# One layer of a hybrid recurrent backbone: the order of HGRN's logarithms, and a power on GpSimd for two token norms

## The chip, the cores and the metric

The kernel runs on one core of one Trainium2 chip. The metric is the device time of one execution in microseconds (us). The engines are named as in the profile: PE is TensorE's matmuls, PEld its weight loads, DVE is VectorE, ACT is ScalarE, POOL is GpSimd, and SP (SyncE) issues most transfers. PE's clock has two levels, 1.2 and 2.4 GHz; the profile gives the granted clock of a stretch as a share of the higher one.

## The reference

One layer on 640 tokens (128 of context, 512 latent) with 1024 channels: a modulated RMS norm, one wide projection, three recurrent mixers (HGRN2, RWKV-7, mLSTM), a gated merge, an output projection, and a SwiGLU feed-forward block. The change concerns HGRN's forget gates, and the RMS norm of each token over the 128 channels of a head, which HGRN and mLSTM both have:

```python
def _rms(x, w, eps=RMS_EPS):
    x32 = x.astype(F32)
    y = x32 * lax.rsqrt(jnp.mean(x32 * x32, axis=-1, keepdims=True) + eps)
    return (y * w.astype(F32)).astype(x.dtype)
...
    for d, fpre in enumerate((hf_fwd, hf_bwd)):
        z = fpre.astype(F32)
        logf = jnp.logaddexp(log_lb, log_ub + jax.nn.log_sigmoid(z)).reshape(B, T, HA, DKA)
        k = ((1.0 - lb) * jax.nn.sigmoid(-z)).reshape(B, T, HA, DKA)
...
    o = _rms(outs[0] + outs[1], norm_w.reshape(HA, DVA)).reshape(B, T, WA)
    return o * jax.nn.silu(hg.astype(F32)), jnp.stack(finals, axis=1)
...
    h = _rms(hs[0] + hs[1], norm_w.reshape(HC, DHC)).reshape(B, T, WC)
    return h * jax.nn.sigmoid(mo.astype(F32)), (jnp.stack(Cs, axis=1), jnp.stack(ns, axis=1), jnp.stack(ms, axis=1))
```

Both mixers have four heads of 128 channels, each run in both directions of time (fwd and bwd).

## The kernel before, in words

Channels lie on the partitions and the 640 tokens along the free axis, in two halves of 320; where a step needs tokens on the partitions, PE transposes blocks of 128x128 (`htr`, `hotr`, `mhtr`, `btr`). A projection multiplies in split floats: ACT casts a piece of a weight to its high part (`whi`, L344), DVE makes the low part (`wlo`, L262), and PE runs three products for each block of 128 channels (`pj<-h_hi,whi`, `h_lo,whi`, `h_hi,wlo`, all in the helper `mm`, L277). Four pairs of `whi` and `wlo` exist at a time; their sources `raw` are loaded by SP (`wload`, L332).

The stages, by their place in the span: modulation and the first norm up to 40 us; RWKV to about 605; the gates of mLSTM; from about 620 to 1010 the four heads of HGRN and of mLSTM, side by side; the merge with `ya`, `yc` and `hl` to 1100; the output projection with its norm (`rstd_rows`, L1519) to about 1235; the feed-forward block; the last norm.

In the stage of the heads two generators, `mlstm()` and `hgrn()`, are woven, a step of one after some steps of the other, and `fill()` lays projections between them that nothing in the heads waits for: the gates (their evacuation is L572, a Tanh, from PSUM to `gs`; L573 writes `gs` to DRAM, one half at a time, and two `gs` exist) and a part of the modulation of the next block (`acc`, `col`). `FILL2` sets how much fill goes to each head. The program order that comes out of this is a priority only: a list scheduler places the instructions on each engine in a fixed order before the kernel runs, by when it reckons their inputs to be there, and on the chip each engine keeps that order, an instruction waiting in front of all behind it. `tc.issue_after(x)` adds one rule to the scheduler: on x's engine what stands in the block comes after x. A table load of ACT is put in where two neighbours in ACT's final order need different tables.

A head of HGRN (`hgrn_head`): projections, then for each direction the gate's logarithm through Abs, Exp and Ln (L1096 to L1100), k through an Exp (L1107), a scan (L1110), Exps for the chunk states (`kh` L1118, `hqe` L1121, `heb` a copy on POOL); the transposes `htr`, their copy `hkt` (L1138), the states `hpr`; seven levels of pairs of Exp (`T1`, `T2`, L1193 and L1194, whose inputs POOL and DVE subtract, L1189 on) with products `hg`; the output `hop`, its copy to `o` and the sums of squares by ACT (L1222, `hssq`, 128 tokens by 5 chunks), the root and the reciprocal (L1223, L1224), the scaling of the five chunks (L1226), the transposes `hotr` (L1236), and `ya`, its high part by ACT (L1052) and its low part by DVE.

A head of mLSTM (`mlstm_head`): projections, `mkt` (L558, the copy of k's transposes), products `ms`, an Exp (`mD`, L1367), numerators `np` and `nq`, their copy `nd` (L1394), the division, sums of squares (L1413, `ssq`), root and reciprocal (L1414, L1415), the scaling (L1417), the transposes `mhtr` and `yc`.

Of the kernel before, what the change touches and what calls it, by code (L numbers as in the profile page):

```python
# [8 lines left out]
F32 = mybir.dt.float32  # L9
# [3 lines left out]
AF = mybir.ActivationFunctionType  # L13
ALU = mybir.AluOpType
# [88 lines left out]
COL_EPS6, COL_EPS64, COL_9LN2, COL_SEL = 0, 1, 2, 3  # L103
# [152 lines left out]
def build(tc, **A):  # L256
    nc = tc.nc
    dve, act, pe, pool, sp = nc.vector, nc.scalar, nc.tensor, nc.gpsimd, nc.sync
# [8 lines left out]
    def stt(out, a, s, b, op0, op1):  # L267
        dve.scalar_tensor_tensor(out, a, s, b, op0, op1)

    def ts(out, a, s1, s2=None, op0=ALU.mult, op1=ALU.add):  # L270
        if s2 is None:
            dve.tensor_scalar(out, a, s1, None, op0)
        else:
            dve.tensor_scalar(out, a, s1, s2, op0, op1)  # L274
# [18 lines left out]
    with ExitStack() as top:  # L293
# [22 lines left out]
        def col(i):  # L316
            return cols[:, i:i + 1]

        def P(n, i=0, w=1):
            return pcol[:, PC[n] + i:PC[n] + i + w]  # L320
# [724 lines left out]
        with ExitStack() as ms, ExitStack() as mr:  # L1045
# [18 lines left out]
            hb = ms.enter_context(tc.tile_pool(name="hb", bufs=1, reuse_waits="tile"))  # L1064
# [8 lines left out]
            ts(lb[:, 1], lb[:, 1], -1.0, 1.0)  # L1073
            rub = hb.tile([128, 4], F32, name="rub")
            dve.reciprocal(rub, lb[:, 1])
            hhn = hb.tile([128, 4], F32, name="hhn")
            ts(hhn, P("hn", 0, 4), 0.5)

            def hgrn_head(hd):
# [8 lines left out]
                b, kd, qe, SSs, zs, ls, khs, ebs = [], [], [], [], [], [], [], []  # L1088
# [5 lines left out]
                for d in D2:  # L1094
                    l = ht.tile([128, T], F32, name="hT2")
                    act.activation(l, zs[d], AF.Abs)  # L1096
                    act.activation(l, l, AF.Exp, scale=-1.0)
                    ls.append(l)
                for l in ls:
                    act.activation(l, l, AF.Ln, scale=rub[:, hd:hd + 1], bias=rub[:, hd:hd + 1])  # L1100
                yield
                for d in D2:
                    kk_ = hb.tile([128, T], F32, name=f"hk{d}")
                    bb = hb.tile([128, T], F32, name=f"hb{d}")
                    l = ls[d]
                    stt(kk_, zs[d], 0.0, l, ALU.max, ALU.add)
                    act.activation(kk_, kk_, AF.Exp, scale=-1.0)  # L1107
                    stt(l, zs[d], 0.0, l, ALU.min, ALU.subtract)
                    st = 1 if d == 0 else -1
                    dve.tensor_tensor_scan(bb[:, ::st], r128, l[:, ::st], 0.0, ALU.mult, ALU.add)  # L1110
                    b.append(bb)
                    kd.append(kk_)
                    yield
# [95 lines left out]
                ssq = hb.tile([128, 5], F32, name="hssq")  # L1209
                sq = hb.tile([128, 128], F32, name="hsq")  # L1210
                for c0, n in CP:
# [8 lines left out]
                    act.copy(o[:, c0:c0 + n], op[:, :n])  # L1220
                    for i in range(n):
                        act.activation(sq, op[:, i], AF.Square, accum_out=ssq[:, c0 + i:c0 + i + 1])  # L1222
                act.activation(ssq, ssq, AF.Sqrt, scale=1.0 / 128, bias=col(COL_EPS6))  # L1223
                dve.reciprocal(ssq, ssq)  # L1224
                for c in range(5):
                    (pool if c in HSP else dve).tensor_scalar(o[:, c], o[:, c], ssq[:, c:c + 1], None, ALU.mult)  # L1226
                hgr = ht.tile([128, T], F32, name="hT2")
# [106 lines left out]
            def mlstm():  # L1334
                yield from mlstm_gates()
                mr.close()
                mt = ms.enter_context(tc.tile_pool(name="mt", bufs=2, reuse_waits="tile"))
                for hd in range(4):
                    at[0] = hd
                    yield from mlstm_head(hd, mt)  # L1340

            def mlstm_head(hd, mt):
# [65 lines left out]
                ssq = mt.tile([128, 5], F32, name="ssq")  # L1408
                sq = mt.tile([128, 128], F32, name="msq")
                for c in range(5):  # L1410
                    ts(hh[:, c], nds[0][:, c, 0:128], rds[0][:, c:c + 1])
                    stt(hh[:, c], nds[1][:, c, 0:128], rds[1][:, c:c + 1], hh[:, c], ALU.mult, ALU.add)
                    act.activation(sq, hh[:, c], AF.Square, accum_out=ssq[:, c:c + 1])  # L1413
                act.activation(ssq, ssq, AF.Sqrt, scale=1.0 / 128, bias=col(COL_EPS6))  # L1414
                dve.reciprocal(ssq, ssq)  # L1415
                for c in range(5):
                    ts(hh[:, c], hh[:, c], ssq[:, c:c + 1])  # L1417
                og = mt.tile([128, T], F32, name="og", bufs=1)
# [11 lines left out]
            def hgrn():  # L1430
                for hd in range(4):
                    yield from hgrn_head(hd)
# [399 lines left out]
```

## Time and profile before

| what | value |
| --- | --- |
| median of 3 runs | 1620.4 us (1620.4 to 1620.68) |
| the profiled execution, its time | 1623.08 us |
| its span, first to last instruction | 1621.3 us |
| mean granted clock | 0.976 |
| PE busy | 1540.6 us, 95% of the span |
| DVE, ACT, POOL busy | 1131.9, 782.8, 275.7 us |

The span leaves out 1.8 us around the first and the last instruction. "Busy" counts an instruction from start to end, overlaps once; "idle before" is how long its engine stood, and the name behind the arrow is the instruction that ended it. Matmuls overlap, so a start says more about PE's pace than a duration does: neighbouring `pj` matmuls start 0.147 us apart at the full clock.

### The profile page before, as it was taken

To read this page: it belongs to the slowest core of one execution; us is meant where nothing else is said; L and a number is where in the kernel's file an instruction comes from. 1 tells how busy PE (TensorE), PEld (TensorE's weight loads), DVE (VectorE), ACT (ScalarE), POOL (GpSimd) and SP (SyncE) were. 2 spreads that over 40 slices of the span, in tenths; PEclk is the share of its full clock that TensorE was granted. 3 is DMA by queue.
4 is the path that set the end of the run, shared out by engine and by line. 5 is a ranking of instruction groups with operands and counts; after the bars stand their busy time and mean duration, and the time that the engine had idled before them with its cause. 6 is when DMAs were issued, how large, how long until landed. Compare 5 with 4: busy or idle time off the path is not lost. (4 is left out here: it accounts for less than half of the span.)

```text
span 1621.3 us, 34724 instructions
## 1 busy us (share of the span) xinstructions
PE 1540.6 (95%) x14194; PEld 1418.1 (87%) x14194; DVE 1131.9 (70%) x2355; ACT 782.8 (48%) x1546; POOL 275.7 (17%) x347
## 2 busy tenths in 40 slices
PE   6999999999999988899999999999999999999996
PEld 2988888888877778889798988999999999999996
DVE  6788788687777644786758578772887386586576
ACT  5364455454454334666476666223553343243244
POOL 2110110110110100211303031000123241341211
PEclk9999999999999969999999999999989999999998
DMA  9222222212122313232332332643512222222322
GB/s 361 71 75 88 74 71 80 95 50 88 66 73 95 113 49 103 70 99 78 94 100 85 100 101 95 201 145 108 155 37 86 95 79 76 82 88 68 99 94 97
DMA packets 63791, 157.35 MB, mean 97 GB/s; under 512 B 7432, under 2 KB 27912, under 8 KB 63504
## 3 DMA queue, kind: packets, MB, share of 16 engines
q1 hardware_dynamic: 63488, 155.13, 29.5%
q8 instruction: 111, 1.82, 0.5%
q14 instruction: 48, 0.39, 0.1%
q10 hardware_dynamic: 144, 0.00, 0.0%
HBM read 136.73 MB, written 18.37 MB: 96 GB/s over the span
## 5 line engine op out<-in xcount | busy, mean ns | idle before, releaser
L277 PE MATMUL pj<-h_hi,whi 128*128 128x320 f32 x1560 | 495.0, 320 | 5.4 <-ACT t L396 2.7
L277 PE MATMUL pj<-h_lo,whi 128*128 128x320 f32 x1560 | 494.4, 317 | 0.0
L277 PE MATMUL pj<-h_hi,wlo 128*128 128x320 f32 x1560 | 493.2, 317 | 0.0
L262 DVE TENSOR_TENSOR wlo<-raw,whi 128x512 fp32r<-128x512 f32 (+1 forms) x318 | 228.5, 726 | 130.7 <-ACT whi L344 106.2
L277 PEld LDWEIGHTS pj<-h_hi,whi 128*128 128x128 f32 x1560 | 296.3, 191 | 12.0 <-ACT t L396 3.7
L277 PEld LDWEIGHTS pj<-h_lo,whi 128*128 128x128 f32 x1560 | 296.7, 190 | 3.2
L277 PEld LDWEIGHTS pj<-h_hi,wlo 128*128 128x128 f32 x1560 | 296.9, 190 | 2.8
L344 ACT CAST whi<-raw 128x512 fp32r<-128x512 f32 (+1 forms) x264 | 156.8, 599 | 219.6 <-PE pj L277 209.4
L277 PE MATMUL pj<-a,whi 128*128 128x320 f32 x704 | 155.3, 309 | 0.0
L277 PEld LDWEIGHTS pj<-a,whi 128*128 128x128 f32 x704 | 117.7, 188 | 0.2
L277 PE MATMUL pj<-a,wlo 128*128 128x320 f32 x352 | 108.8, 309 | 0.0
L277 PE MATMUL pj<-t_hi,whi 128*128 128x320 f32 x288 | 89.1, 309 | 1.1 <-DVE u L262 1.1
L277 PE MATMUL pj<-t_hi,wlo 128*128 128x320 f32 x288 | 89.1, 309 | 0.1
L277 PE MATMUL pj<-t_lo,whi 128*128 128x320 f32 x288 | 89.0, 309 | 0.0
L262 DVE TENSOR_TENSOR wlo<-sm,whi 128x512 fp32r<-128x512 f32 x72 | 68.1, 946 | 11.4 <-ACT whi L1684 8.5
L1684 ACT CAST whi<-sm 128x512 fp32r<-128x512 f32 x72 | 44.4, 621 | 64.4 <-PE pj L277 50.2
L1678 POOL TENSOR_TENSOR sm<-raw 128x512 f32<-128x512 f32 x36 | 49.0, 1360 | 110.3 <-DMA raw<-wff 72.5
L277 PEld LDWEIGHTS pj<-a,wlo 128*128 128x128 f32 x352 | 66.1, 188 | 0.0
L277 PE MATMUL pj<-hl,whi 128*128 128x320 f32 x256 | 56.5, 310 | 0.6 <-ACT hl L1462 0.6
L1684 ACT CAST whi<-raw 128x512 fp32r<-128x512 f32 x54 | 33.5, 620 | 45.6 <-PE pj L277 37.7
L277 PEld LDWEIGHTS pj<-t_hi,whi 128*128 128x128 f32 x288 | 54.1, 188 | 1.3 <-DVE u L262 1.3
L277 PE MATMUL acc<-raw,sc 128*32 128x256 f32 (+1 forms) x320 | 40.7, 437 | 14.8 <-DMA raw<-wada 14.8
(659 smaller groups left out, 2988.0 us busy)
## 6 DMA issues: line engine op xcount, KB each, us to landing
raw<-wmix SPq DMA_DIRECT2D x76, 512.0 KB, 3.5
raw<-wada SPq DMA_DIRECT2D x48, 512.0 KB, 5.6
raw<-wff SPq DMA_DIRECT2D x44, 512.0 KB, 3.7
gates<-gs SPq DMA_DIRECT2D x64, 160.0 KB, 1.8
raw<-wff SPq DMA_DIRECT2D x24, 384.0 KB, 3.2
gs<-gates SPq DMA_DIRECT2D x24, 320.0 KB, 3.1
raw<-wbr SPq DMA_DIRECT2D x12, 512.0 KB, 4.3
raw<-wout SPq DMA_DIRECT2D x8, 512.0 KB, 5.0
```

What stands on the lines that cost most here:

```text
L262: dve.tensor_tensor(out, a, b, op)
L277: newest[0] = pe.matmul(out, lhsT=lhsT, rhs=rhs, start=start, stop=stop, skip_group_check=more).ins
L344: act.copy(hi[:, :w], raw[:, o:o + w])
L1678: pool.tensor_tensor(o, x, y, op)
L1684: act.copy(hi, x)
```

## The change

The first part is in HGRN's gate. Before, the two Ln are placed by the scheduler as their inputs come, each direction for itself, with other Exps between. Now both Ln may only follow the second direction's Exp (L1099 in the new numbering), and each Exp of hk (now L1112) only the second Ln. The second part is in both norms: `ssq` becomes `ssq`/128 + 1e-6 by a tensor_scalar on DVE, and POOL raises it to the power of a tile `mhalf` that holds -0.5, a tensor_tensor with the operation pow over 128x5. ACT's Sqrt (128x5) and DVE's reciprocal (128x5) go. `mhalf` is filled once by POOL.

```diff
             rub = hb.tile([128, 4], F32, name="rub")
             dve.reciprocal(rub, lb[:, 1])
+            mhalf = hb.tile([128, 5], F32, name="mhalf")
+            pool.memset(mhalf, -0.5)
...
                     act.activation(l, zs[d], AF.Abs)
-                    act.activation(l, l, AF.Exp, scale=-1.0)
+                    last = act.activation(l, l, AF.Exp, scale=-1.0).ins
                     ls.append(l)
-                for l in ls:
-                    act.activation(l, l, AF.Ln, scale=rub[:, hd:hd + 1], bias=rub[:, hd:hd + 1])
+
+                with tc.issue_after(last):
+                    for l in ls:
+                        last = act.activation(l, l, AF.Ln, scale=rub[:, hd:hd + 1], bias=rub[:, hd:hd + 1]).ins
                 yield
...
-                    act.activation(kk_, kk_, AF.Exp, scale=-1.0)
+                    with tc.issue_after(last):
+                        act.activation(kk_, kk_, AF.Exp, scale=-1.0)
...
-                act.activation(ssq, ssq, AF.Sqrt, scale=1.0 / 128, bias=col(COL_EPS6))
-                dve.reciprocal(ssq, ssq)
+                ts(ssq, ssq, 1.0 / 128, 1e-6)
+                pool.tensor_tensor(ssq, ssq, mhalf, ALU.pow)
                 for c in range(5):
                     (pool if c in HSP else dve).tensor_scalar(o[:, c], o[:, c], ssq[:, c:c + 1], None, ALU.mult)
...
-                act.activation(ssq, ssq, AF.Sqrt, scale=1.0 / 128, bias=col(COL_EPS6))
-                dve.reciprocal(ssq, ssq)
+                ts(ssq, ssq, 1.0 / 128, 1e-6)
+                pool.tensor_tensor(ssq, ssq, mhalf, ALU.pow)
                 for c in range(5):
                     ts(hh[:, c], hh[:, c], ssq[:, c:c + 1])
```

The lines of the new program are 2 to 5 higher than those of the old one for the same step. The scheduler places much of the stage of the heads anew. Three places:

ACT in head 0, from the second direction's `hqe` (the Exp of `hb`) to the copy `hkt`: L1118 and L1123 are the Exp of `kh`, L1193/L1194 and L1198/L1199 the Exps of T1 and T2. Before:

```order
L1121 ACTIVATE hqe_9011<-hb_8931 128x640
L396 ACTIVATE mq<-pj 128x320
L344 CAST whi<-raw 128x512
L1118 ACTIVATE hT_9007<-hT_9007 128x640
L1193 ACTIVATE hT_9124<-hT_9124 128x640
L1194 ACTIVATE hT_9125<-hT_9125 128x640
L396 ACTIVATE mk<-pj 128x320
L344 CAST whi<-raw 128x512
L1194 ACTIVATE hT_9199<-hT_9199 128x640
L1194 ACTIVATE hT_9235<-hT_9235 128x640
L396 ACTIVATE mk<-pj 128x320
L1138 COPY hkt<-htr 128x512
```

and now:

```order
L1126 ACTIVATE hqe_9013<-hb_8933 128x640
L396 ACTIVATE mk<-pj 128x320
L1198 ACTIVATE hT_9126<-hT_9126 128x640
L1123 ACTIVATE hT_9009<-hT_9009 128x640
L344 CAST whi<-raw 128x512 x2
L396 ACTIVATE mk<-pj 128x320
L1143 COPY hkt<-htr 128x512
L1198 ACTIVATE hT_9200<-hT_9200 128x640
L1199 ACTIVATE hT_9127<-hT_9127 128x640
L1199 ACTIVATE hT_9201<-hT_9201 128x640
```

Three Exps of T2 stood ahead of the copy; now they stand behind it.

PE at the end of head 0, where the five transposes `hotr` of HGRN's output stand among the fill (`pj`). Before, 21 fill matmuls come between the last `nq` of mLSTM and the first `hotr`; these are the last of them and what follows:

```order
L277 MATMUL pj<-h_lo,whi 128x320
L277 MATMUL pj<-h_hi,wlo 128x320
L277 MATMUL pj<-h_hi,whi 128x320
L277 MATMUL pj<-h_lo,whi 128x320
L1236 MATMUL hotr<-cst,hT_9477 128x128 x2
L277 MATMUL pj<-h_hi,wlo 128x320
L1236 MATMUL hotr<-cst,hT_9477 128x128 x2
L277 MATMUL pj<-h_hi,whi 128x320
L1236 MATMUL hotr<-cst,hT_9477 128x128
```

and now the whole way from that `nq` on:

```order
L277 MATMUL nq<-Cs,mq 128x129
L277 MATMUL pj<-h_hi,wlo 128x320
L277 MATMUL pj<-h_hi,whi 128x320
L277 MATMUL pj<-h_lo,whi 128x320
L277 MATMUL pj<-h_hi,wlo 128x320
L277 MATMUL pj<-h_hi,whi 128x320
L277 MATMUL pj<-h_lo,whi 128x320
L277 MATMUL pj<-h_hi,wlo 128x320
L277 MATMUL pj<-h_hi,whi 128x320
L1241 MATMUL hotr<-cst,hT_9479 128x128
```

Eight fill matmuls stand there instead of 21.

SP's queue in head 1, at the two gate transfers (`gates<-gs`) ahead of the state that HGRN writes out (`ohg`). Before:

```order
L332 DMA raw<-wmix 128x1024 x6
L573 DMA gates<-gs 128x320
L332 DMA raw<-wmix 128x1024
L573 DMA gates<-gs 128x320
L1147 DMA ohg<-hfs 128x128
```

and now:

```order
L332 DMA raw<-wmix 128x1024 x4
L573 DMA gates<-gs 128x320
L332 DMA raw<-wmix 128x1024
L573 DMA gates<-gs 128x320
L332 DMA raw<-wmix 128x1024
L1152 DMA ohg<-hfs 128x128
```

Each of the two gate transfers has passed one weight load, which now follows it.

## Rows read from the trace of the kernel before

**Rows 1.** The page's head, and busy time, share of the span and instructions of PE, PEld, DVE, ACT and POOL.

```profile
span 1621.3 us, 34724 instructions
PE 1540.6 (95%) x14194; PEld 1418.1 (87%) x14194; DVE 1131.9 (70%) x2355; ACT 782.8 (48%) x1546; POOL 275.7 (17%) x347
```

**Rows 2.** Busy time by stretches of 20 us through the stage of the heads: length; PE, PEld, DVE, ACT and POOL busy with their instructions; granted clock, DMA share, GB/s. The last row is the sum of all twenty from 620 to 1020.

```profile
640.00:660.00 20.00, 20.00 (x140) 19.99 (x139) 10.19 (x12) 14.60 (x24) 1.67 (x2) 1.00 0.25 79
...
720.00:740.00 20.00, 19.94 (x140) 19.50 (x139) 11.12 (x32) 13.77 (x30) 0.00 (x0) 1.00 0.33 108
...
sum 400.00, PE 380.29 PEld 358.69 DVE 282.36 ACT 246.81 POOL 71.95; mean PE 19.01 PEld 17.93 DVE 14.12 ACT 12.34 POOL 3.60
```

**Rows 3.** PE's waits from 620 to 1030: what waited, for whom; us in total, times, the longest.

```profile
PE nq L277 <- ACT nd L1394: 5.8, 6, 1.5
PE hpr L277 <- ACT hkt L1138: 5.4, 3, 5.0
PE ms L277 <- ACT mkt L558: 3.5, 3, 1.5
PE pj L277 <- DVE mod L262: 0.7, 1, 0.7
```

**Rows 4.** Groups of ACT's instructions by line and operation: busy time, mean ns of one, idle before.

```profile
L1100 ACT ACT_TABLE_LOAD x8 | 10.3, 1283 | 0.1
L1107 ACT ACT_TABLE_LOAD x8 | 10.3, 1283 | 0.1
...
L1223 ACT ACT_TABLE_LOAD x4 | 5.1, 1283 | 0.1
L1414 ACT ACT_TABLE_LOAD x4 | 5.1, 1283 | 0.1
L572 ACT ACT_TABLE_LOAD x4 | 5.1, 1283 | 0.4 <-DMA gates<-gs 0.4
```

**Rows 5.** ACT's timeline in head 0: start, duration, what, and the idle time before it with what ended it.

```profile
649.18 1.28 ACT L1100 ACT_TABLE_LOAD   x1
650.48 0.92 ACT L1100 ACTIVATE hT<-hT,rub 128x640 f32<-128x640 f32 x1
...
668.94 0.74 ACT L1194 ACTIVATE hT<-hT 128x640 f32<-128x640 f32 x1 [1.63 <-DVE hT L262]
...
672.33 1.54 ACT L1194 ACTIVATE hT<-hT 128x640 f32<-128x640 f32 x2 [1.82 <-DVE hT L262]
...
674.09 0.58 ACT L1138 COPY hkt<-htr 128x512 f32<-128x512 f32 x1
```

**Rows 6.** PE's longest wait in head 0, from its timeline, and two stretches of 2 us around it (columns as in Rows 2).

```profile
674.73 0.58 PE L277 MATMUL hpr<-hv,hkt 128*128 128x128 f32 x1 [4.96 <-ACT hkt L1138]
...
672.00:674.00 2.00, 0.00 (x0) 0.00 (x0) 2.00 (x5) 1.60 (x3) 0.00 (x0) 0.55 0.00 0
...
676.00:678.00 2.00, 2.00 (x10) 2.00 (x10) 1.16 (x4) 0.00 (x0) 0.00 (x0) 0.50 0.45 84
```

**Rows 7.** Timelines around `mkt`: SP's queue and ACT in head 1, then PE's first `ms` in heads 1, 2 and 3. For SP the duration is how long the transfer's issue stood in the queue.

```profile
765.23 7.30 SPq L332 DMA_DIRECT2D raw<-wmix  x2
772.62 0.38 SPq L573 DMA_DIRECT2D gates<-gs  x1
...
776.58 0.44 ACT L572 ACTIVATE gs<-pj 128x320 f32<-128x320 f32 x1 [2.61 <-DMA gates<-gs]
...
777.44 0.38 PE L277 MATMUL ms<-mq,mk 128*128 128x128 f32 x1 [1.47 <-ACT mkt L558]
869.64 0.38 PE L277 MATMUL ms<-mq,mk 128*128 128x128 f32 x1 [0.53 <-ACT mkt L558]
962.23 0.38 PE L277 MATMUL ms<-mq,mk 128*128 128x128 f32 x1 [1.52 <-ACT mkt L558]
```

**Rows 8.** Timelines at the end of head 0: the last read of a sum of squares and the table load on ACT; HGRN's scaling and mLSTM's reciprocal on DVE; on PE the eighth fill matmul behind the last `nq`, and the first `hotr`.

```profile
719.10 0.28 ACT L1222 ACTIVATION_READ_ACCUMULATOR hsq<-hop 128x1 f32 x1
...
719.90 1.28 ACT L1223 ACT_TABLE_LOAD   x1
...
721.88 1.06 DVE L1226 TENSOR_SCALAR hT<-hT,hssq 128x128 f32<-128x128 f32 x5
...
729.12 0.19 DVE L1415 RECIPROCAL ssq<-ssq 128x5 f32<-128x5 f32 x1 [2.36 <-ACT ssq L1414]
...
720.03 0.31 PE L277 MATMUL pj<-h_hi,whi 128*128 128x320 f32 x1
...
722.30 0.43 PE L1236 MATMUL hotr<-cst,hT 128*128 128x128 f32 x2
```

**Rows 9.** POOL: groups by line and shape (busy time, mean ns of one, idle before), and from its timeline the first tensor_tensor of the kernel.

```profile
L1189 POOL TENSOR_TENSOR hT<-hb 128x320 f32<-128x320 f32 x28 | 27.7, 990 | 95.4 <-PE htr L1136 43.5 <-DVE hT L268 15.6 <-ACT hfs L1146 9.5
...
L1373 POOL TENSOR_TENSOR vs<-v,TM 128x645 f32<-128x645 f32 x8 | 11.4, 1429 | 189.4 <-ACT v L558 186.3 <-PE kv L277 3.1
...
L1123 POOL COPY heb<-hqe 128x5 f32<-128x5 f32 x8 | 2.1, 267 | 4.2 <-ACT hqe L1121 4.2
...
31.15 0.86 POOL L494 TENSOR_TENSOR h_lo<-xT,h_hi 128x320 fp32r<-128x320 f32 x1
```

**Rows 10.** PE's two waits in the stage of the output projection, at the sums of squares `ss` of the norm, from its timeline.

```profile
1144.76 0.59 PE L277 MATMUL ss<-ones,S 128*80 128x1 f32 x6 [2.01 <-DVE S L1579]
...
1179.79 0.42 PE L277 MATMUL ss<-ones,S 128*80 128x1 f32 x4 [1.87 <-DVE S L1579]
```

## The prediction

> **What bounds the kernel now.** I read the busy times first: TensorE (PE) is at work for 1540.6 of 1621.3 us, 95% [rows 1]. ScalarE (ACT), which the change relieves, is under half. So ACT's time counts only where PE stands and waits for it. The table by stretches says where that is not: in a slice that holds a head's logarithms (640 to 660) PE is busy for 20.00 of 20 us, and in one that holds both roots of a head (720 to 740) for 19.94 [rows 2]. In the whole stage of the heads (620 to 1020) PE is busy 380.29 of 400 us, so 19.7 us are all that could be won there [rows 2]. Third, the view of PE's waits tells for whom it stands: for `nd` 5.8 us (a copy behind mLSTM's products, far from any table load), for `hkt` 5.4, for `mkt` 3.5, and 0.7 once for `mod` [rows 3]. The last view is each engine's timeline around those waits [rows 5 to 8].
>
> The forecast is made against the profiled execution: 1621.3 us of span and 1.8 around it, 1623.1, which lies 2.7 over the median of 1620.4. What I find is taken off the median.
>
> **What is removed from ACT.** Each load of a table takes 1.283 us, and the instruction after it starts at once [rows 4, 5]. Before, a head pays two at the logarithms' line and two at the Exp of hk, and one each at the two Sqrt lines and at L572 behind them [rows 4]. The order of instructions has 54 loads before and 32 after: 8 at Ln and Exp, 8 at the Sqrts, 4 at L572, 3 elsewhere go, and one is new, at the first Sqrt of `rstd_rows`. So 22 x 1.283 = 28.2 us of ACT go; besides, 8 Sqrts and 8 reciprocals on VectorE (DVE) become 8 tensor_scalars and 8 powers on GpSimd (POOL).
>
> The Trainium skill (ScalarE: Activation LUTs, section "Table sets: the hidden batching unit") has one set with both exp and ln. By that rule the four functions of a head would need no load between them, and the first half of the change would free nothing; by the rows it frees 8 x 1.283 = 10.3 us of ACT. The rows decide, since the trace shows a load at each of them [rows 4].
>
> Of these 28.2 us nearly all are covered: in the slices where they stand PE has 0.00 and 0.06 us idle [rows 2]. The cover is the fill, gate projections issued between the heads' steps. What can be won is what ACT's shift does to PE's waits.
>
> *Head 0, `hkt`.* PE waits 4.96 us for a copy that starts at 674.09 though its input, four transposes, was done when PE fell idle, at 674.73 - 4.96 = 669.8 [rows 5, 6]. It stands behind two groups of Exp that themselves wait for DVE, 1.63 and 1.82 us [rows 5]. In the new order (the ACT fence above) the copy stands ahead of all three of those Exps, behind two weight casts and an evacuation. Following the instructions by their durations, I have it end at about 673.2 instead of 674.7, so some 1.5 us go, and 0.2 for work moved by PE: 1.7, no more, since DVE stays full in those microseconds. The granted clock, 0.55 and 0.50 behind this gap [rows 6], I expect to fall as before, because 3.2 us of gap stay.
>
> *Heads 1 and 3, `mkt`.* PE waits 1.47 and 1.52 us [rows 7]. In head 1 ACT sits in front of it, at L572, for a transfer of `gates<-gs`, which SP issued only at 772.62: a weight load ahead of it stood in SP's queue for 7.30 us [rows 7]. In the new order the gate transfer is ahead of that load (the SP fence), so it goes out as soon as its data is there, near 771.5, and L572 no longer waits. I take all of it: 1.5 twice. Head 2's 0.53 [rows 7] I count at 0.3, since its queue keeps its order. Two DMAs change place there and are otherwise the same.
>
> *End of the heads.* The last head has three table loads in the last 8 us before the merge; without them the casts come over a microsecond sooner, but PE's wait there is 0.7 [rows 3], with two smaller ones beside it: I count 0.7.
>
> Sum of the gains: 1.7 + 1.5 + 1.5 + 0.3 + 0.7 = 5.7 us.
>
> **What is added.** The scheduler now puts the five `hotr` transposes 13, 12, and 13 matmuls earlier in the first three heads (the PE fence), right behind 7 or 8 fill matmuls. Before, PE reached them at 722.30 and never waited; now it does so at about 720.18, after the start at 720.03 [rows 8]. Its input must pass five steps: the last sum of squares ends at 719.38 [rows 8], a tensor_scalar of 128x5 takes about 0.19, as the reciprocal does [rows 8], then the power, d, then the first scaling, 1.06 / 5 = 0.21 [rows 8], with some 0.05 between engines. That is 719.38 + 0.05 + 0.16 + 0.05 + d + 0.05 + 0.24 = 719.9 + d. PE waits d - 0.25 for the first, and up to 0.15 more for the rest: d - 0.1 a head.
>
> No row shows a power. Bounds: a copy of 128x5 on POOL takes 0.27; tensor_tensors take 0.99 at 320 and 1.43 at 645 elements a partition [rows 9], so (1.43 - 0.99) / 325 = 1.35 ns each and about 0.55 for almost none. A power is more work per element than a subtraction; from five elements I take d = 0.8, nearer to 0.55 than to 1.43, and keep 0.27 to 2 for the range (no row bounds it above). POOL is idle there (x0 from 720 to 740 [rows 2]). So 4 x 0.7 = 2.8 us are lost, 0.7 to 7.6 at the ends.
>
> During that wait DVE is blocked at the scaling, and behind it stand `hk`, `rd` and a weight's low half. Before, it stood 2.36 us for the Sqrt of `ssq` [rows 8], with a low half behind it, and PE did not notice; the same cover holds. For `ssq`, 33 to 47 fill matmuls lie ahead of `mhtr` in these heads; its chain ended at 729.12 + 0.19 = 729.31 [rows 8], after a load of 1.28 [rows 4], a Sqrt and the reciprocal, 1.5 at least; a tensor_scalar, d and two crossings make 1.1, so it ends no later than before. I put 0.3 for head 2, where the distance is shortest.
>
> In `rstd_rows` the new load (1.28) is on the way to the first `rr`, which has 10 more matmuls ahead of it; PE's two waits for `S`, 2.01 and 1.87 [rows 10], become about 1.3 and 3.1 as 5 matmuls join one and 8 leave the other: 0.5 lost. Before 612 us and in the FFN no row moves.
>
> Sum: -5.7 + 2.8 + 0.3 + 0.5 = -2.1 us: 1621.0 in a profile, 1618.3 on the median. Own range 1614.5 to 1622.
>
> **Rivals.**
> *A, the power is slow.* One mechanism: d at 2 us. Then `hotr` waits 4 x 1.9 = 7.6, and a gap that long can take the clock down as `hkt`'s does: a slice at 0.50 loses 1 us of 2 [rows 6], and with a part of the next one I take 1.35 a head, 5.4. With 5.2 won elsewhere (5.7 - 0.5): +7.8, 1628. It beats the gains from 4 x (d - 0.1) + 0.8 = 5.7, d = 1.3. For it: no row shows the function. Against: five elements only.
>
> *B, first call.* The first power alone takes 6 us or so, the others 0.8: 5.2 + 1.35 for the clock, so -2.1 + 6.6 = +4.5, 1625. From the trace: the first tensor_tensor on POOL takes 0.86, no more than the later ones [rows 9], so a first use costs nothing there; but another function may. The Trainium skill (GPSIMD Engine Reference, section 2.1) states about 6 us for the first call of a freshly loaded routine; that is this rival's rule, and the first tensor_tensor's row doesn't bear it out.
>
> *C, everything is hidden or shifted.* The waits for `hkt` and `mkt` go to the next late engine (DVE is busy for 2.00 of 2 us beside the first [rows 6]), and half of the gains (2.9) stay: 2.9 against 3.6, +0.7, 1621.
>
> *D, more is won.* `hkt` and `mkt` go whole, 8.9 us [rows 3], the clock doesn't fall, 1.4, the end gives 1.3 with its smaller waits, and d is 0.27, 0.7 in all for `hotr`, with 0.5 later: -10.4, 1610. For it: ACT has 28 us less to do. Against: DVE is full at that place.
>
> **Numbers.** Forecast 0.50, A 0.16, B 0.05, C 0.12, D 0.17. A difference under 0.2% (3.2 us) can't be told from none. Of the forecast's half, 0.23 is faster than 1617.2, 0.25 within, 0.02 slower; C is 0.09 within, 0.03 slower; D faster, A and B slower. So faster 0.40, within 0.34, slower 0.26. The range leaves out part of A and of D: 1610 to 1627.
>
> **What would show it.** In the new profile: 32 table loads; `hpr<-hkt` of head 0 down to about 3.2 us with the clock still falling; `ms<-mkt` under 0.4 in heads 1 and 3; a new wait `hotr` for DVE of some 0.7 us, four times, and on DVE one for POOL of d; two unequal waits `ss<-S`. A power over 1.3 us, or a clock that falls at `hotr`, makes the prediction wrong on one side; PE busy over 388 of the 400 us makes it wrong on the other.

## The result, and the profile after

The changed kernel takes 1639.7 us at the median (1636.1 to 1642.5) against 1620.4: a ratio of 1.0118, interval 1.0097 to 1.0139, so some 19 us slower. The forecast was 1618.3 in a range of 1610 to 1627. Single executions of one kernel differ by several us, and a part of that is the clock in stages that no edit touches: the way to mLSTM's first wait (`btr` for `hT`, the end of a wait of 4.15 to 4.17 us in all of them) took 609 to 618 us over the fourteen profiles of this study. So profiles are compared from that wait to the end: 1621.3 - 612.4 = 1008.9 us before, and 1640.7 - 614.8 = 1025.9 after (the profiled execution took 1642.5). One execution of the study, of the kernel called "held" below, took 2802 us at a mean clock of 0.934 and is in none of the figures.

The page after, first lines (as in [rows 1]):

```profile
span 1640.7 us, 34714 instructions
PE 1548.4 (94%) x14194; PEld 1424.6 (87%) x14194; DVE 1124.8 (69%) x2355; ACT 755.8 (46%) x1516; POOL 293.8 (18%) x356
```

ACT is 27.0 us less busy, nearly the 22 x 1.283 = 28.2 of the loads that went, and the kernel is slower. The loads that are left at the places in [rows 4] and in `rstd_rows` (L1528), with POOL's powers and its copies of 128x5 (columns as in [rows 4, 9]), and the last power of mLSTM by itself:

```profile
L1104 ACT ACT_TABLE_LOAD x4 | 5.1, 1283 | 0.1
L1112 ACT ACT_TABLE_LOAD x4 | 5.1, 1283 | 0.1
L1528 ACT ACT_TABLE_LOAD x2 | 2.6, 1283 | 0.0
...
L1128 POOL COPY heb<-hqe 128x5 f32<-128x5 f32 x8 | 8.5, 1067 | 33.9 <-ACT hqe L1126 32.2 <-DVE hqe L262 1.7
...
L1420 POOL TENSOR_TENSOR ssq<-ssq,mhalf 128x5 f32<-128x5 f32 x4 | 5.2, 1294 | 29.0 <-DVE ssq L274 29.0
L1229 POOL TENSOR_TENSOR hssq<-hssq,mhalf 128x5 f32<-128x5 f32 x4 | 4.7, 1179 | 24.8 <-DVE hssq L274 24.8
...
1022.07 1.67 POOL L1420 TENSOR_TENSOR ssq<-ssq,mhalf 128x5 f32<-128x5 f32 x1 [7.90 <-DVE ssq L274]
```

A power of 128x5 takes 1.18 us on average in HGRN's norm and 1.29 in mLSTM's, not 0.8: seven of the eight take 1.17 to 1.20, the last one 1.67. PE's waits from 620 to 1060 (columns as in [rows 3]):

```profile
PE hpr L277 <- ACT hkt L1143: 6.9, 5, 1.7
PE nq L277 <- ACT nd L1399: 5.8, 6, 1.5
PE hotr L1241 <- DVE hT L1231: 4.1, 4, 1.2
PE ms L277 <- ACT mkt L558: 2.0, 1, 2.0
PE pj L277 <- DVE mod L262: 1.5, 1, 1.5
PE pj L277 <- DVE wlo L262: 1.2, 1, 1.2
PE mhtr L1432 <- DVE mh L272: 1.2, 1, 1.2
PE pj L277 <- ACT hl L1467: 1.2, 1, 1.2
PE btr L557 <- ACT mk L396: 1.2, 1, 1.2
...
PE col__13213 L277 <- ACT rows L587: 0.5, 1, 0.5
```

`hotr` and `mhtr` are new, as are `wlo` and `mk`; `mkt` went down from 3.5, and `hkt` up from 5.4 [rows 3]. Where they are, from PE's timeline: head 0 (`wlo`, `hkt`, `hotr`), head 1 (two `hkt`, `hfs`), head 2 (`mk`, `mkt`, `mh`).

```profile
672.77 0.42 PE L277 MATMUL pj<-h_hi,wlo 128*128 128x320 f32 x1 [1.25 <-DVE wlo L262]
675.46 2.07 PE L277 MATMUL hpr<-hv,hkt 128*128 128x128 f32 x8 [1.69 <-ACT hkt L1143]
722.77 0.30 PE L1241 MATMUL hotr<-cst,hT 128*128 128x128 f32 x1 [1.19 <-DVE hT L1231]
777.70 1.16 PE L277 MATMUL hpr<-hv,hkt 128*128 128x128 f32 x8 [0.98 <-ACT hkt L1143]
781.80 1.16 PE L277 MATMUL hpr<-hv,hkt 128*128 128x128 f32 x8 [1.61 <-ACT hkt L1143]
783.48 1.23 PE L277 MATMUL hg__10289<-hT,hT 128*64 128x64 f32 x20 [0.52 <-ACT hfs L1151]
874.07 0.44 PE L557 MATMUL btr<-cst,mk 128*128 128x128 f32 x2 [1.16 <-ACT mk L396]
878.20 0.94 PE L277 MATMUL ms<-mq,mk 128*128 128x128 f32 x6 [1.95 <-ACT mkt L558]
924.09 0.33 PE L1432 MATMUL mhtr<-cst,mh 128*128 128x128 f32 x1 [1.20 <-DVE mh L272]
```

Head 0 has 1.25 + 1.69 = 2.9 us in place of 4.96 [rows 6]. Heads 1 and 3 have 0.98 + 1.61 + 0.52 = 3.1 each, where `ms` had 1.47 and 1.52 [rows 7]. Why `hkt` is late in head 1 stands on DVE, twenty microseconds earlier. Its first instructions on the logarithm, after, and the stretches in which it stands:

```profile
758.70 0.82 DVE L268 SCALAR_TENSOR_TENSOR hk<-hT,hT 128x640 f32<-128x640 f32 x1 [3.93 <-ACT hT L1104]
...
740.00:760.00 20.00, 20.00 (x140) 19.99 (x139) 4.72 (x7) 11.35 (x20) 1.27 (x1) 1.00 0.28 79
760.00:780.00 20.00, 19.02 (x135) 18.37 (x133) 19.48 (x29) 13.91 (x25) 8.69 (x6) 1.00 0.21 68
```

and the same of the kernel before, in which head 1 begins 2.3 us earlier:

```profile
748.87 0.82 DVE L268 SCALAR_TENSOR_TENSOR hk<-hT,hT 128x640 f32<-128x640 f32 x1 [3.42 <-ACT hT L1100]
...
740.00:760.00 20.00, 20.00 (x140) 20.00 (x139) 11.14 (x13) 16.55 (x25) 1.66 (x2) 1.00 0.23 77
760.00:780.00 20.00, 18.29 (x128) 17.08 (x126) 15.95 (x27) 13.02 (x25) 6.68 (x7) 1.00 0.32 96
```

DVE's work on the first direction starts 9.8 us later, 7.5 without the shift. It did 11.14 us of work before 760 and now does 4.72; what it missed is packed into the next stretch, 19.48 of 20, and `hkt` comes out of that. How much of the cost this delay carries by itself, a run without the loads shows below.

In the norm of the output projection PE waits at these places, after, and then for `h_hi` before (its two waits for `S` before are in [rows 10]):

```profile
1165.34 0.73 PE L277 MATMUL ss<-ones,S 128*80 128x1 f32 x8 [1.62 <-DVE S L1584]
1199.66 0.85 PE L277 MATMUL ss<-ones,S 128*80 128x1 f32 x8 [2.32 <-DVE S L1584]
1205.43 1.97 PE L277 MATMUL pj<-h_hi,whi 128*128 128x320 f32 x6 [1.41 <-ACT h_hi L1598]
...
1186.46 1.97 PE L277 MATMUL pj<-h_hi,whi 128*128 128x320 f32 x6 [0.87 <-ACT h_hi L1593]
```

PE's waits in all these places, at the end of the heads and in this norm make up 26.1 us after and 15.6 before: 10.5 of the 17.0 between the profiles. The rest goes with the clock. Three stretches after, one in each of heads 1 to 3; before, the clock is 1.00 from behind head 0's fall to the last microseconds of the heads (680 to 1003 us) in both profiles of that kernel:

```profile
784.00:786.00 2.00, 2.00 (x22) 1.65 (x22) 1.56 (x6) 0.00 (x0) 1.15 (x2) 0.50 0.14 39
...
880.00:882.00 2.00, 2.00 (x24) 1.77 (x24) 1.87 (x6) 0.27 (x1) 0.00 (x0) 0.50 0.11 33
978.00:980.00 2.00, 1.98 (x24) 1.87 (x24) 1.59 (x6) 0.00 (x0) 0.64 (x1) 0.55 0.15 41
```

### The profile page after: what moved, and what is told of

Its sections match the earlier page's. It is cut to its first block, busy times and chain, and to the rows that moved or that the text cites. A ratio compares the mean times of both kernels' runs of the same rounds, so it can differ in the third digit from the quotient of the medians.

```text
span 1640.7 us, 34714 instructions
## 1 busy us (share of the span) xinstructions
PE 1548.4 (94%) x14194; PEld 1424.6 (87%) x14194; DVE 1124.8 (69%) x2355; ACT 755.8 (46%) x1516; POOL 293.8 (18%) x356
## 5 line engine op out<-in xcount | busy, mean ns | idle before, releaser
L277 PEld LDWEIGHTS pj<-t_hi,wlo 128*128 128x128 f32 x288 | 54.1, 188 | 0.6 <-DVE wlo L262 0.6
```

Source lines behind the costliest of these rows:

```text
L277: newest[0] = pe.matmul(out, lhsT=lhsT, rhs=rhs, start=start, stop=stop, skip_group_check=more).ins
```

## Experiments

Theory A: the logarithms held together cost most, by the late start of the first direction. Its rival B: the power and the new place of `hotr`. All edits are against the kernel before unless said.

**The logarithms alone, and the norms alone.** Each half of the change, as in its diff; the first:

```diff
+                with tc.issue_after(last):
+                    for l in ls:
+                        last = act.activation(l, l, AF.Ln, scale=rub[:, hd:hd + 1], bias=rub[:, hd:hd + 1]).ins
...
+                    with tc.issue_after(last):
+                        act.activation(kk_, kk_, AF.Exp, scale=-1.0)
```

> The order of the logarithms alone, norms as in the kernel before. Theory A (holding the first direction's Ln behind the second direction's Exp starts that direction's whole chain on VectorE some 7 us later, VectorE stands idle and is then packed, and PE waits at hkt and mkt and loses its clock in heads 1 to 3): 1630 us, 8 to 13 over before; in the profile the first hk on VectorE comes 7 us later in each head, the clock falls in heads 1, 2 and 3, and hotr waits for nothing. Rival B (the power and the new place of hotr carry nearly all of the 19 us): within 3 us of before, 1618 to 1623, and no fall of the clock in heads 1 to 3.

the second:

```diff
+                ts(ssq, ssq, 1.0 / 128, 1e-6)
+                pool.tensor_tensor(ssq, ssq, mhalf, ALU.pow)
```

> The power on GpSimd alone, logarithms as in the kernel before. Theory A: the power takes 1.2 us, hotr waits 1.2 us four times and mhtr once, the three waits at ms and hpr stay, and the clock keeps its level in heads 1 to 3: 1625 us, 4 to 7 over before. Rival B: 1633 us or more.

The logarithms: 1627.8 us, ratio 1.0044 (1.0029 to 1.0060), 8 us over the 1619.6 of its kernel before. The norms: 1634.3, 1.0086 (1.0070 to 1.0102), 14.7 over. The first fits A's figure at its lower end, the second is B's figure: neither theory holds alone, the norms are the larger half, and 8 and 10 to 15 us (the second run of the norms is below) add up to about the whole change's 19. In the first, PE waits for `hkt` in heads 1 and 3 as in the whole change:

```profile
773.45 1.16 PE L277 MATMUL hpr<-hv,hkt 128*128 128x128 f32 x8 [0.98 <-ACT hkt L1141]
777.55 1.16 PE L277 MATMUL hpr<-hv,hkt 128*128 128x128 f32 x8 [1.61 <-ACT hkt L1141]
...
963.13 1.16 PE L277 MATMUL hpr<-hv,hkt 128*128 128x128 f32 x8 [0.98 <-ACT hkt L1141]
967.23 1.16 PE L277 MATMUL hpr<-hv,hkt 128*128 128x128 f32 x8 [1.61 <-ACT hkt L1141]
```

The clock, though, fell in head 2 alone of heads 1 to 3. In the second, `hotr` waits 4.1 us in all and `mhtr` 1.2, and the clock keeps its level in heads 1 to 3 in this profile. It did not in the second profile of the same kernel ("both again", below), in which it fell in heads 2 and 3:

```profile
882.00:884.00 2.00, 2.00 (x10) 2.00 (x9) 2.00 (x5) 0.32 (x2) 0.00 (x0) 0.51 0.04 6
...
966.00:968.00 2.00, 2.00 (x10) 1.78 (x12) 1.77 (x5) 0.77 (x2) 0.00 (x0) 0.50 0.01 2
```

**A reciprocal, or a multiplication, in the power's place.** Both against the norms alone: on DVE, with no other engine crossed; and on POOL, with the same crossings and the same order of instructions on PE, ACT, DVE and POOL:

```diff
-                pool.tensor_tensor(ssq, ssq, mhalf, ALU.pow)
+                dve.reciprocal(ssq, ssq)
```

> As the power alone, but VectorE's reciprocal stands in place of GpSimd's power (the norm is then by the mean square and not by its root): ScalarE's root and its table loads are gone as in the change, and no engine is crossed. Theory A: hotr waits under 0.3 us, 1618 to 1622 us, so what the run with the power loses beyond that is the power's length. If the loss came from moving hotr forward or from ScalarE's new pace, it would be 1625 us again.

```diff
-                pool.tensor_tensor(ssq, ssq, mhalf, ALU.pow)
+                pool.tensor_tensor(ssq, ssq, mhalf, ALU.mult)
```

> The power alone, with a multiplication in the power's place on GpSimd (the norm's factor is then another): the same crossings of engines and the same order of instructions. If the power's own length is the cost, the multiplication takes 0.2 to 0.5 us, hotr waits 0.2 to 0.5 instead of 1.2, and the time is 1625 to 1628 us. If crossing to GpSimd is the cost whatever it computes, it stays at 1632 or more.

The reciprocal: 1624.5, ratio 1.0027 (1.0018 to 1.0037), no wait at `hotr`. That is outside the 1618 to 1622 that I expected and beside the rival's 1625. The multiplication: 1626.0, 1.0027 (1.0010 to 1.0045), as expected; it takes 0.33 us and `hotr` waits 0.6 in all:

```profile
L1417 POOL TENSOR_TENSOR ssq<-ssq,mhalf 128x5 f32<-128x5 f32 x4 | 1.3, 326 | 29.0 <-DVE ssq L274 29.0
...
PE hotr L1238 <- DVE hT L1228: 0.6, 3, 0.2
```

So the power's own length is a large part of the norms' loss: with the multiplication 5.8 us are left of 14.7 in the first run of the norms and of 10.2 in the second, and PE's waits at `hotr` and `mhtr` fall from 5.3 to 0.8. But 4 to 6 us stay even without it. Of these the traces show a part: in the run with the reciprocal, the norm of the output projection, whose first Sqrt has the new table load, waits 1.70 + 2.49 at `ss`, against 2.01 + 1.87 [rows 10], and 1.40 for `h_hi` instead of 0.87; the first product with `ya` waits 1.57 for `mod` instead of 0.7 [rows 3]. In the run with the multiplication such waits, with what is left at `hotr` and `mhtr`, make 3.0 us more than before. The rest is open: whether it is `hotr`'s new place, ScalarE's new pace or the clock, no run tells apart, and the reciprocal's profile took 1008.9 us from the wait for `hT` to the end, as long as the first one of the kernel before.

**No table loads at the logarithms.** An Exp for the Ln, once with each direction free to go, once held as in the change (both have PE's order of the logarithms alone, instruction for instruction):

```diff
-                    act.activation(l, l, AF.Ln, scale=rub[:, hd:hd + 1], bias=rub[:, hd:hd + 1])
+                    act.activation(l, l, AF.Exp, scale=rub[:, hd:hd + 1], bias=rub[:, hd:hd + 1])
```

> The kernel before with an Exp in place of the Ln of the logarithms (so the gate's values are others): the four functions of a head need no table load between them, as the change wants, and each direction still goes when its inputs come. Theory A: the loads' removal by itself costs nothing, and the chain of the first direction starts 2 us earlier, not 7 later: 1615 to 1620 us. If a lighter ScalarE itself brought the packing (the rival to the delay), this would be 5 us or more over before.

> The order of the logarithms as the change holds it, norms as before, and an Exp in place of the Ln (so the gate's values are others): no table load at the logarithms at all, PE's order that of the logarithms alone. Theory A (the holding costs, wherever the loads lie): VectorE's first hk again comes 6 to 8 us late in each head, 1623 to 1629 us, 5 to 10 over the same kernel without the holding (1618.0). Rival C (the two loads that remain, standing side by side ahead of both directions, are what delays): under 1620.

Free: 1618.0, ratio 0.9979 (0.9970 to 0.9989), a little faster than before. Held: 1619.9, 1.0000 (0.9987 to 1.0012), a miss: I expected 1623 to 1629, and by a hair it is the figure of rival C there. A lighter ScalarE does not hurt, and neither does PE's new order, so neither is the cause of this half's loss. The holding by itself costs 1.9 us over the free one, though PE waits for `hkt` in heads 1 and 3 here too:

```profile
769.65 1.16 PE L277 MATMUL hpr<-hv,hkt 128*128 128x128 f32 x8 [1.91 <-ACT hkt L1141]
```

With its two loads and the Ln it costs 1627.8 - 1619.9 = 7.9 more. From the wait for `hT` to the end the two profiles took 1006.5 and 1013.3 us; of these 6.8, PE's waits are 3.0 (27.7 and 30.8 in all), and the rest goes with the clock. Read from the timelines of head 1, in us from the first Abs to the start of DVE's first scan, its second scan, and the two copies `hkt`:

| kernel | first scan | second scan | `hkt` | `hkt` |
| --- | --- | --- | --- | --- |
| before | 5.98 | 14.96 | 28.30 | 33.09 |
| no loads, free | 4.21 | 12.79 | 29.76 | 32.08 |
| no loads, held | 12.93 | 14.34 | 30.63 | 33.14 |
| logarithms alone | 13.67 | 16.52 | 29.71 | 33.82 |
| the change | 13.66 | 16.52 | 29.70 | 33.81 |

Before, there are four loads a head, but those of the first direction come while PE is still at the second one's projection, and those of the second while DVE has the first: little waits for them, as the first scan comes only 1.8 us sooner without them. Held, there are two, the first ahead of both Ln and so ahead of all that DVE has to do, the second ahead of both Exps of hk. The table shows the late first scan with and without the loads (13.67 and 12.93); what the loads and the Ln add is at the second scan, which then comes 2.9 us behind the first instead of 1.4, and at the second `hkt`.

The free run says one thing more. Its waits for `mkt` in heads 1 and 3 are gone, but PE stands there 1.0 and 1.1 us for `hkt` and 0.9 for `hfs` instead: 2.0 a head, where it was 1.8 for `mkt`, `hkt` and `hfs` together before.

**One power at a time, and both again.** In mLSTM's norm alone, in HGRN's alone, and the norms alone a second time:

> The power on GpSimd in mLSTM's norm alone; HGRN's norm and the logarithms as before. hotr keeps its 19 to 21 fill matmuls and waits for nothing; mhtr stands 3 to 11 matmuls earlier and can wait up to 1 us in one or two heads. Theory A (the cost of the norm's half is the power in front of a transpose that stands too early, so above all HGRN's): 1619 to 1624 us. If each power costs alike wherever it stands, half of the norms' loss: 1627.

> The power on GpSimd in HGRN's norm alone; mLSTM's norm and the logarithms as before. Theory A: hotr waits 1.2 us three times and 0.6 once as with both powers, mhtr does not wait, and most of the norms' 14 us is there: 1627 to 1632 us. If the powers cost alike: 1627; if the loss of the norms' half came from the later stages (their one new table load), under 1624.

> Both powers on GpSimd, logarithms as before, once more with more executions. Each power alone cost 3.3 and 5.2 us against the kernel before, both together 14.7 in four executions. If the two simply add, and the rest was chance of those four (in the profiled one the part up to the first wait for hT, which no edit touches, was 5 to 6 us longer than in the kernel before), this is 1627 to 1631 us. If they do more together than apart (PE's waits close enough to take the clock down), it is 1633 to 1636 again, and the time from that wait to the end is 1016 us or more, against 1005 and 1009 in the two profiles of the kernel before.

mLSTM's: 1623.8, 1.0019 (1.0004 to 1.0034), with `mhtr` waiting 0.34, 0.96 and 1.30. HGRN's: 1625.7, 1.0031 (1.0020 to 1.0043), `hotr` 4.1, a little under the 1627 to 1632 that I expected. Both again: 1630.2, 1.0070 (1.0049 to 1.0091). The halves, 3.3 and 5.2 us, make 8.5 beside 10.2 here and 14.7 the first time. By the median this is the sum that I had named (1627 to 1631). By the other sign it is not: from the wait for `hT` to the end the profile took 1018.3 us (1016.6 in the first run), over the 1016 that I had named for more than a sum, where the two halves took 1010.7 and 1011.9. So they add up but for 1.7 us by the second run's median and 6.2 by the first's, and whether the two powers do that together stays open. In the first run's profile the part up to the wait for `hT` had taken 5.8 us more than in the first one of the kernel before, with the clock down from 115 to 125 among other places:

```profile
120.00:130.00 10.00, 10.00 (x100) 9.41 (x99) 6.10 (x13) 3.44 (x6) 0.00 (x0) 0.75 0.04 16
```

**The logarithms held in head 0 alone,** the head where the change shortened PE's wait:

```diff
+                with tc.issue_after(last) if hd == 0 else ExitStack():
...
+                    with tc.issue_after(last) if hd == 0 else ExitStack():
```

> The logarithms held together in head 0 alone, the other three heads and all norms as before. Theory A: head 0 is the one head where the holding shortened PE's wait (4.96 us for hkt became 1.69 and 1.25 for a weight's low half), the other heads' waits return to those of before, so 1616 to 1619 us, 1 to 3 us under the kernel before. If what is held costs wherever it is done, 1621 or more.

1623.6, ratio 1.0014 (1.0002 to 1.0026): a miss. PE's wait shrank as expected (`wlo` 1.23 and `hkt` 1.69 for 4.96), and no time came back; the median even lies 3.1 us over that of the kernel before, though the profile took 1006.3 from the wait for `hT` to the end, between the 1005.1 and 1008.9 of that kernel. In the profile the clock fell behind the shorter wait as behind the longer one, and once more in head 1, at a wait for `mkt` of 1.37 that it did not fall at before.

**The kernel before and the changed one once more,** for a second profile of each:

> The kernel before once more, for a second profile. Up to 612 us nothing differs between any of these kernels, yet that part took 612.4 us in the profile of before, 614.8 in that of the change and 618.2 with the power alone. If this is chance of single executions (the clock falling or not in the first 180 us), this profile shows another value again, 608 to 618, and the time from there to the end stays at 1009 us within 2.

> The changed kernel once more, for a second profile. Theory A: from 612 us (the first wait for hT) to the end it takes 17 us more than before, again within 3, with hotr at 1.2 us a head and the clock falling once in each of heads 1, 2 and 3. If the falls of the clock in the heads are chance, they are fewer or elsewhere, and the time moves by 1 to 1.5 us for each.

Before: 1619.8 us; 613.0 to the wait for `hT` and 1005.1 from there, 3.9 less than the first time, with fewer falls of the clock. After: 1641.1, 614.2 and 1025.2, with the same waits and the clock down once in each of heads 1, 2 and 3 again. So in the changed kernel these falls came in both profiles, and in none of the two of the kernel before.

## Why the prediction was wrong

*Right.* The loads: 32, and 27 us less of ACT hidden. That removing loads wins little: 1618.0 with none at the logarithms. Head 0: 2.9 us and a falling clock, for 3.2, though 1.25 of it is for `wlo`, which I had not named. By luck, the projection's norm: waits grew by 0.6, for 0.5, but the two for `S` kept their sum (3.9), and what grew is the wait for `h_hi`, which I had left out.

*Heads 1 to 3, the step that failed.* "I take all of it: 1.5 twice." The waits for `mkt` did go in heads 1 and 3, and the gate transfers moved as read. But the step looked at ACT and SP only, around the wait, and took the wait that it saw end last for the only one. The free run shows that removing the loads does not win this 1.5: PE then waits for `hkt` and `hfs` in `mkt`'s place, as rival C of the prediction has it. And the step did not ask when DVE gets its first work if the first Ln must stand behind the second direction's Exp. That Exp follows a projection of 48 matmuls, 7.5 us of PE, and then come load, Ln, Ln. So a wait of 3.1 came in heads 1 and 3 where I had 0.2, and in head 2 3.1 instead of 0.6: 5.0 us more than before in these heads, where I had 3.3 less. The holding alone costs 1.9 us (held without loads); I counted the removal of a load as a gain of at least zero, but the two that stayed, with the Ln, carry 7.9 more. The rule of the Trainium skill (ScalarE: Activation LUTs, "Table sets: the hidden batching unit") that exp and ln share a set is not what the traces show: after the change, too, each pair of Ln has its load (L1104), and the Exps behind it another (L1112).

*The power, a term mis-sized.* d is 1.2, not 0.8: `hotr` 4.1 instead of 2.8, `mhtr` 1.2 instead of 0.3. By d alone this is near rival A's break-even of 1.3; but the falls of the clock at `hotr` that rival A counts did not come, and of the 10 to 15 us that the norms alone cost, these waits are only 5.3. Rival B fell: the first power took 1.20 us, no longer than the others. The first call's 6 us or so of the Trainium skill (GPSIMD Engine Reference, section 2.1) is not seen here.

*The end of the heads.* I had 0.7 won; the waits for `rows`, `mod` and `hl` went from 1.5 to 3.1. They are in the run of the norms alone too (`mod` 1.5, `hl` 1.2), so they come from there.

*The clock.* Falls in heads 1 to 3 I priced in rivals A and B alone. In both profiles of the change one came in each of these heads, behind waits of 1 to 2 us in quick succession, and the 17.0 - 10.5 = 6.5 us that the waits leave over go with these and with longer falls behind them. The other kernels had fewer such falls: one with the logarithms alone, none and two in the two profiles of the norms alone. What decides between them the runs do not tell: the clock also fell behind a single wait for `mkt` of 1.37 us (held in head 0 alone) and of 1.61 (the norms again), and before the change it kept its level behind one of 1.47.

*The range.* Single executions of the kernel before went from 1615.9 to 1625.8 over the study, more than the three shown ahead (0.3 us apart). My bound of 0.2% was tighter than a few executions can tell.

## What to carry to other kernels

When work is grouped to save a switch, the group waits for its last member: look at who works while the first member's result is there and the last one's isn't, and whether that engine can make it up later (here it did when no load was left, and did not with two). A saved instruction on an engine with slack is worth little (16 loads less, 20 us of ScalarE, gave 2 to 3 us), and one that is left can become dear if it moves to the head of a chain. An operation that no row shows should be priced with its upper bound wherever the scheduler has put its reader close behind it.

## What the hardware showed that I had not expected

A power of 128x5 on GpSimd takes 1.17 to 1.20 us, once 1.67, where a multiplication of the same shape takes 0.33. The copies `heb` of 128x5 took 0.27 us on average before and 1.07 after, 1.08 with the logarithms alone and 0.24 with the norms alone. The long ones lie in the packed stretch of VectorE, but a busy VectorE alone does not explain them: before, too, VectorE is busy for the whole of a copy of 0.28 us. What makes them four times as long stays open. The clock fell behind waits of 1.4 us in some profiles and not in others of the same places, and in the first 180 us of an unchanged program in some executions only.
